# First attention's outputs stored unnormalised, their scale applied where the first branch loads them

## Chip, core and metric

The kernel runs on one core of a Trainium2 chip. The metric is device time in microseconds (us) of one execution; 2043.49 us is the median of three runs of the kernel before.

## The reference, cut to what matters

One layer of a decoder trunk on 1024 tokens of width 1024, in float32. Three token mixers A, B and C each give 512 features per token. The change touches mixer A, differential attention with four heads of 128 values each:

```python
s = jnp.einsum('bqhcd,bkhcd->cbhqk', qi, k) * scale + bias
p = jax.nn.softmax(jnp.where(mask, s, NEG_INF), axis=-1)
w = p[0] - lam * p[1]
oa = jnp.einsum('bhqk,bkhe->bqhe', w, v)
...
oa = (rms_norm(oa, diff_subln[layer]) * (1.0 - lam_init)).reshape(B, S, MIX_WIDTH)
...
y = jnp.einsum('nbsm,nmd->bsnd', branches, w_branch[layer])
gate = jax.nn.sigmoid(mg.reshape(B, S, N_BRANCH, D_MODEL))
x = x + jnp.sum(gate * y, axis=2) @ w_out[layer]
```

`rms_norm` divides each token's 128 values of a head by the root of their mean square. A per-value gain (`diff_subln`) and a constant follow.

## The kernel before

The work runs in stages on one core. Five engines work in their own order: TensorE (PE, with its weight loads PEld), VectorE (DVE), ScalarE (ACT), GpSimd (POOL) and SyncE (SP), which issues nearly all DMAs. PE's order is the order in which the code is written; the other engines' orders are set by a scheduler that simulates the program. Each engine then takes its instructions strictly in order.

Matrix products are made from a high and a low part of each operand (`split`: ScalarE copies the high part, L90, and DVE or POOL subtracts it, L91), three matmuls for each product (`mm3`, L118 to L120).

`run` goes through the stages. `mix` weaves two streams of PE work: a fine one, the steps of an attention (`pipeline`, `step`), and a dense one, the matmuls of a projection or of gates. First attention (mixer A, four heads, `items_a`) is woven with the projections of the next head. An item is a block of 256 queries of one head, so 16 items in all. Each step makes logits (L711), exponentials (`expo`, L743), transposes of the probabilities into a PSUM bank (`pblocks`, L759), and products with the values that gather in a bank `ac`.

PSUM gives two banks named `tr` in turn to whoever asks: the attention's transposes (L759), the projection's transposes (`to_state`, L558, copied out by DVE in L564 or ScalarE in L562), and the end of an item. That end works as follows. `values` copies the item's output `o`, value dimension on the partitions, out of PSUM (L861). Some steps later `by_token` (L869 to L882) transposes it to token on the partitions (L872), copies it (L874), takes each token's sum of squares (L878), adds the epsilon that was scaled by the softmax's sum (L879), raises it to the power -0.5 on POOL (L880) and multiplies (L881). Again two steps later `by_feature` (L884 to L890) transposes back (L887), applies `subln` in the copy (L889) and stores 128x256 to `od` in DRAM. The helper `late` holds these two for a number of steps.

Mixers B and C follow. The second half of mixer C's attention (`items_c`, g = 1) is woven with `first_branch`: for each half of the tokens some gates (`gates(n)`), the loads of mixer A's four heads from `od` (`operand`, L1130, then `split` to `xh`, `xl`), some more gates (`gates(m)`), and eight products with the branch's weights (`branch`), each gated and stored to `yd`. Gates go to DRAM by L1124. In this stage raw loads have two buffers (`wr`), weight parts four (`wh`, `wl`), and the tile pool `sq` still holds the projection's small tiles `y` with two buffers.

Of the kernel before, what the change touches and what calls it, by code (L numbers as in the profile page):

```python
# [11 lines left out]
F32 = mybir.dt.float32  # L12
F32R = mybir.dt.float32r
AF = mybir.ActivationFunctionType
ALU = mybir.AluOpType
AX = mybir.AxisListType

P = 128
S = 1024
# [56 lines left out]
class Kernel:  # L76
# [97 lines left out]
    def run(self):  # L174
        tc, nc, a = self.tc, self.nc, self.a
# [25 lines left out]
        self.w_n, self.wr_bufs, self.w_bufs = 396, WR, 8  # L201
        self.od = self.dram.tile([12, P, S], F32, name="od")
        self.gd = self.dram.tile([24, P, S], F32, name="gd")
        self.yd = self.dram.tile([KT, P, S], F32, name="yd")
        self.next_gate = 0
        self.mm, self.alone, self.raws = self.sc, True, []
# [112 lines left out]
    def idents(self):  # L319
        nc = self.nc  # L320
        self.cst.tile([P, 24], F32, name="gap0")
        self.ident = self.cst.tile([P, P], F32, name="ident")
        make_identity(nc, self.ident)
        self.identr = self.ca.tile([P, P], F32R, name="identr")
        nc.vector.tensor_copy(self.identr, self.ident)
        self.nhalf = self.cst.tile([P, 8], F32, name="nhalf")
        nc.vector.memset(self.nhalf, -0.5)
        self.cst.tile([P, 120], F32, name="gap1")
        self.gk = self.ca.tile([P, 3, HD], F32, name="gk")
        self.gsw = self.ca.tile([P, 2, HD], F32, name="gsw")  # L330

# [457 lines left out]
    def items_a(self, h, sta):  # L789
        nc, at = self.nc, self.at  # L790
        bias = self.bias[:, h, :]
        for qb in range(4):
            pq = [None, None]
            box = {}
# [48 lines left out]
            rows = []  # L843
# [9 lines left out]
            def values(i, ph, pl, kt, qb=qb, box=box):  # L853
                if kt + i == 0:
                    box["ac"] = self.ac()
                self.mm3(box["ac"], sta["v"][:, kt + i, 0, :], sta["v"][:, kt + i, 1, :], ph, pl,
                         kt + i == 0, kt + i == 2 * qb + 1)
                if kt + i == 2 * qb + 1:
                    box["o"] = at.tile([P, 256], F32, name="o1", tag="o1", bufs=2)
                    with self.tc.high_priority(offset=self.urgent):  # L860
                        nc.scalar.activation(box["o"], box["ac"], AF.Copy)  # L861
                return 0.33

            groups = [self.group(lambda j, kt, pq=pq: pq[j][:, kt * P:(kt + 1) * P], qb, (kt, kt + 1),
                                 lambda t, kt: kt <= t, lambda i, ph, pl, kt=kt, values=values: values(i, ph, pl, kt))
                      for kt in range(0, 2 * qb + 2, 2)]


            def by_token(box=box, qb=qb):  # L869
                pt = self.tr()  # L870
                for j in range(2):
                    nc.tensor.transpose(pt[:, j * P:(j + 1) * P], box["o"][:, j * P:(j + 1) * P], self.ident)  # L872
                o2 = box["o2"] = at.tile([P, 2, P], F32, name="o2", tag="o2", bufs=2)
                nc.scalar.activation(o2, pt[:, 0:256].rearrange("p (j e) -> p j e", e=P), AF.Copy)  # L874
                ss = at.tile([P, 2, 2], F32, name="sso", tag="sso", bufs=2)
                for j in range(2):
                    v = pt[:, j * P:(j + 1) * P]
                    nc.scalar.activation(v, v, AF.Square, accum_out=ss[:, 0, j:j + 1])  # L878
                nc.vector.scalar_tensor_tensor(ss[:, 1, :], ss[:, 0, :], 1.0 / P, box["eps"], op0=ALU.mult, op1=ALU.add)  # L879
                nc.gpsimd.tensor_tensor(ss[:, 1, :], ss[:, 1, :], self.nhalf[:, 0:2], op=ALU.pow)  # L880
                nc.vector.tensor_tensor(o2, o2, ss[:, 1, :].unsqueeze(2).to_broadcast([P, 2, P]), op=ALU.mult)  # L881
                self.late.append([2, lambda: by_feature(box, qb)])  # L882

            def by_feature(box, qb):  # L884
                pt = self.tr()
                for j in range(2):
                    nc.tensor.transpose(pt[:, j * P:(j + 1) * P], box["o2"][:, j, :], self.ident)  # L887
                o1 = at.tile([P, 256], F32, name="o1", tag="o1", bufs=2)
                nc.scalar.activation(o1, pt[:, 0:256], AF.Copy, scale=self.subln)  # L889
                nc.sync.dma_start(self.od[h, :, qb * 256:(qb + 1) * 256], o1)  # L890

            yield dict(rows=rows, groups=groups, end=[by_token])

    def head_values(self, box, dst, v, ph, pl, first, last):

# [228 lines left out]
                nc.sync.dma_start(self.gd[f, :, hs], o)  # L1124


    def operand(self, src, s, hi, lo):

        raw = self.wp.tile([P, 512], F32, name="wr", tag="wr", bufs=self.wr_bufs)
        self.nc.sync.dma_start(raw, src[:, s])  # L1130
        self.split(hi, lo, raw)


# [14 lines left out]
    def first_branch(self):  # L1148
        nc = self.nc
        for half, n, m in ((0, GATES[3], GATES[4]), (1, GATES[5], 24 - sum(GATES))):  # L1150
            s = slice(half * 512, half * 512 + 512)
            yield from self.gates(n)
            o = [self.parts(tag="x") for _ in range(4)]
            for i in range(4):
                self.operand(self.od[i], s, *o[i])
            yield from self.gates(m)
            for d in range(KT):
                w = self.weight(self.a["wbr"][0, d], 512)
                g = self.gate(self.sq, "tm", 2, 0, d, s)
                ps = self.branch(0, d, [x[0] for x in o], [x[1] for x in o], w)  # L1160
                with self.tc.high_priority(offset=self.urgent):
                    nc.vector.scalar_tensor_tensor(g, g, 1.0, ps, op0=ALU.add, op1=ALU.mult)
                nc.sync.dma_start(self.yd[d, :, s], g)
                yield 2.6
# [424 lines left out]
```

## Time and profile before

| | |
|---|---|
| runs, us | 2043.49, 2041.05, 2048.14 (median 2043.49) |
| profiled execution, us | 2045.69 |
| its span, first to last instruction | 2043.7 |
| mean granted TensorE clock | 0.98 |
| TensorE busy | 1901.7 us, 93% |
| DVE, ScalarE, POOL busy | 70%, 50%, 47% |

| stretch, us | stage |
|---|---|
| 0 to 160 | norm, first projection, compression of keys for mixer C |
| 160 to 455 | first attention (mixer A) with the projections |
| 455 to 870 | mixer B, first half of mixer C, with projections and gates |
| 870 to 1196 | second half of mixer C with gates and first branch |
| 1196 to 2044 | other branches, output product, MLP |

A row of a group reads: line, engine, operation, output tile <- input tiles, shape, count | busy us in all, mean ns of one | idle time of the engine just before them and what ended it. A row of a timeline begins with start and length in us. PE's matmuls overlap, so what one of them costs is the distance between starts, not its shown length.

### The profile page before, as it was taken

Reading aid. Unit: us, or ns where it says so; the run is one execution under the profiler, and the core shown is the slowest. Engines: PE = TensorE matmul, PEld = TensorE weight load, DVE = VectorE, ACT = ScalarE, POOL = GpSimd, SP = SyncE. Lnnn points to the kernel's source line nnn. Section 1 sums busy time; section 2 is a strip of 40 time slices with the busy share of each in tenths; the row PEclk is TensorE's granted clock in tenths of the full one; section 3 lists DMA queues with packets and bytes.
Section 4 is the critical chain, followed back from the end, with each engine's and each line's share of the span. In section 5 each row is a group of like instructions: output and inputs, shape, how many; then the busy total and the mean of one; then the engine's idle time right before and its main releaser. Section 6 shows DMA issues by size and latency. Waiting matters only on the chain. (4 is left out here: it accounts for less than half of the span.)

```text
span 2043.7 us, 30701 instructions
## 1 busy us (share of the span) xinstructions
PE 1901.7 (93%) x9838; PEld 1621.5 (79%) x9838; DVE 1423.4 (70%) x3231; ACT 1022.0 (50%) x2626; POOL 954.3 (47%) x1142
## 2 busy tenths in 40 slices
PE   7999888988799999999999899999899998999998
PEld 6888887888688888887888677787688886888876
DVE  6757777788848677648676755657755544889898
ACT  5456556666636555536555533335455544444331
POOL 4455355544352212162222227218444445789784
PEclk9999999999999999999999899999899998999999
DMA  5131022011211111212242456425444446355343
GB/s 218 51 104 52 4 55 59 26 38 37 87 28 61 56 52 51 72 33 91 68 147 77 159 198 204 147 93 161 172 167 160 144 145 247 119 167 163 124 144 114
DMA packets 122558, 219.49 MB, mean 107 GB/s; under 512 B 14420, under 2 KB 35412, under 8 KB 122396
## 3 DMA queue, kind: packets, MB, share of 16 engines
q1 hardware_dynamic: 120812, 211.75, 31.9%
q10 hardware_dynamic: 1584, 5.77, 0.9%
q8 instruction: 78, 1.28, 0.3%
q14 instruction: 84, 0.69, 0.1%
HBM read 156.59 MB, written 64.81 MB: 108 GB/s over the span
## 5 line engine op out<-in xcount | busy, mean ns | idle before, releaser
L91 POOL TENSOR_TENSOR wl<-wr,wh 128x512 fp32r<-128x512 f32 (+3 forms) x246 | 328.8, 1343 | 275.0 <-ACT wh L90 238.8
L90 ACT ACTIVATE wh<-wr 128x512 fp32r<-128x512 f32 (+3 forms) x258 | 150.3, 590 | 183.8 <-PE mm L119 124.1
L711 PE MATMUL sc<-st 128*128 128x256 f32 (+5 forms) x736 | 183.9, 344 | 25.9 <-ACT p L743 25.3
L90 ACT ACTIVATE ph<-tr 128x384 fp32r<-128x384 f32 (+3 forms) x280 | 138.4, 497 | 105.5 <-PE tr L759 87.0
L91 DVE TENSOR_TENSOR pl<-tr,ph 128x384 fp32r<-128x384 f32 (+3 forms) x280 | 155.8, 559 | 40.2 <-ACT ph L90 37.6
L756 POOL MEMSET ph<- 128x128 f32 x152 | 35.7, 235 | 291.3 <-PE ac L901 253.0
L711 PEld LDWEIGHTS sc<-st 128*128 128x128 f32 x736 | 122.8, 192 | 47.5 <-ACT p L743 38.8
L118 PE MATMUL mm<-hh,wh 128*128 128x512 f32 x384 | 158.8, 414 | 0.0
L120 PE MATMUL mm<-hh,wl 128*128 128x512 f32 x384 | 151.5, 395 | 0.0
L119 PE MATMUL mm<-hl,wh 128*128 128x512 f32 x384 | 151.4, 394 | 0.0
L119 PE MATMUL mm<-wl,wh 128*128 128x512 f32 x352 | 139.5, 396 | 9.4 <-POOL wl L91 9.4
L118 PE MATMUL mm<-wh 128*128 128x512 f32 x352 | 139.9, 398 | 8.2 <-DVE x L1471 5.3
L90 ACT ACTIVATE wh<-u 128x512 fp32r<-128x512 f32 x162 | 93.0, 620 | 106.3 <-PE mm L119 27.9
L759 PE MATMUL tr<-ident,p 128*128 128x128 f32 x792 | 129.2, 275 | 16.9 <-ACT o L889 7.8
L120 PE MATMUL mm<-wh,wl 128*128 128x512 f32 x352 | 139.1, 395 | 0.0
L743 ACT ACTIVATE p<-sc,mc 128x256 f32<-128x256 f32 (+5 forms) x200 | 106.7, 538 | 52.0 <-DVE mc L735 47.0
L901 PE MATMUL ac<-ph,st 128*128 128x256 f32 x392 | 109.8, 298 | 19.4 <-DVE ob L908 11.5
L91 POOL TENSOR_TENSOR wl<-s,wh 128x512 fp32r<-128x512 f32 x64 | 89.5, 1405 | 79.3 <-ACT wh L90 79.3
L118 PE MATMUL mm<-wh,hh 128*128 128x384 f32 (+1 forms) x320 | 117.0, 366 | 0.0
L91 DVE TENSOR_TENSOR wl<-u,wh 128x512 fp32r<-128x512 f32 x98 | 112.5, 1150 | 3.9 <-ACT wh L90 3.9
L902 PE MATMUL ac<-pl,st 128*128 128x256 f32 x392 | 106.5, 292 | 6.5 <-DVE pl L91 5.8
L91 POOL TENSOR_TENSOR wl<-u,wh 128x512 fp32r<-128x512 f32 x64 | 98.8, 1557 | 25.1 <-ACT wh L90 25.0
(311 smaller groups left out, 5771.2 us busy)
## 6 DMA issues: line engine op xcount, KB each, us to landing
ud<-u SPq DMA_DIRECT2D x112, 256.0 KB, 2.2
u<-ud SPq DMA_DIRECT2D x98, 256.0 KB, 3.3
wr<-wu SPq DMA_DIRECT2D x76, 256.0 KB, 2.8
wr<-wd SPq DMA_DIRECT2D x64, 256.0 KB, 2.9
gd<-go SPq DMA_DIRECT2D x48, 256.0 KB, 2.0
g<-gd SPq DMA_DIRECT2D x48, 256.0 KB, 3.2
wr<-wg SPq DMA_DIRECT2D x40, 256.0 KB, 2.7
wr<-wbr SPq DMA_DIRECT2D x40, 256.0 KB, 3.0
```

The source lines that it names most:

```text
L90: nc.scalar.activation(hi, src, AF.Copy)
L91: (eng or nc.vector).tensor_tensor(lo, src, hi.bitcast(F32), op=ALU.subtract)
L118: mm(out, lh, rh, start=first, stop=False, skip_group_check=more)
L119: mm(out, lh, rl, start=False, stop=False, skip_group_check=more)
L120: mm(out, ll, rh, start=False, stop=last, skip_group_check=more)
L711: self.nc.tensor.matmul(ps[:, off:off + k1 - k0], q[:, t * P:(t + 1) * P], k[:, k0:k1], start=i == 0, stop=i == 1)
L743: self.nc.scalar.activation(p, ps, AF.Exp, bias=m, scale=-1.0, accum_out=l)
L756: nc.gpsimd.memset(ph[0:rows, o:o + P].bitcast(F32), 0.0)
L759: nc.tensor.transpose(pt[0:rows, o:o + P], src, self.ident)
L901: nc.tensor.matmul(ac, v, ph, start=first, stop=False)
L902: nc.tensor.matmul(ac, v, pl, start=False, stop=last)
```

## The change

The item's output is stored to `od` as it is, right after it is copied out of PSUM. ScalarE squares it into `o2`, and a function `norms` replaces `by_token` and `by_feature`: two products of the squares with a column of ones give the sums per token, with tokens on the partitions. The epsilon and the power follow as before, and the 256 factors are stored to a new DRAM tile `rd`. `operand` loads the factors' row, spread over all partitions, in two pieces of 256, and one DVE instruction for each piece multiplies the raw operand by `subln` and by the row. `first_branch` puts the four operand loads between the matmuls of `gates(m)`, after every fourth step, where they stood ahead of them.

```diff
+        self.rd = self.dram.tile([4, S], F32, name="rd")
...
+        self.ones = self.cst.tile([P, 8], F32, name="ones")[:, 0:1]
+        nc.vector.memset(self.ones, 1.0)
...
                         nc.scalar.activation(box["o"], box["ac"], AF.Copy)
+                    o2 = box["o2"] = at.tile([P, 256], F32, name="o2", tag="o2", bufs=2)
+                    nc.scalar.activation(o2, box["o"], AF.Square)
+                    nc.sync.dma_start(self.od[h, :, qb * 256:(qb + 1) * 256], box["o"])
...
-            def by_token(box=box, qb=qb):
+            def norms(box=box, qb=qb):
                 pt = self.tr()
                 for j in range(2):
-                    nc.tensor.transpose(pt[:, j * P:(j + 1) * P], box["o"][:, j * P:(j + 1) * P], self.ident)
...
-                self.late.append([2, lambda: by_feature(box, qb)])
...
+                    nc.tensor.matmul(pt[:, j:j + 1], box["o2"][:, j * P:(j + 1) * P], self.ones, start=True, stop=True)
+                ss = at.tile([P, 2], F32, name="sso", tag="sso", bufs=2)
+                nc.vector.scalar_tensor_tensor(ss, pt[:, 0:2], 1.0 / P, box["eps"], op0=ALU.mult, op1=ALU.add)
+                nc.gpsimd.tensor_tensor(ss, ss, self.nhalf[:, 0:2], op=ALU.pow)
+                r = self.rd[h]
+                nc.sync.dma_start(bass.AP(tensor=r.tensor, offset=r.offset + qb * 256, ap=[[1, P], [P, 2]]), ss)
...
+        if rows is not None:
+            for o in (0, 256):
+                r = self.sq.tile([P, 256], F32, name="y", tag="y", bufs=2)
+                src = bass.AP(tensor=rows.tensor, offset=rows.offset + s.start + o, ap=[[0, P], [1, 256]])
+                self.nc.sync.dma_start(r, src)
+                v = raw[:, o:o + 256]
+                self.nc.vector.scalar_tensor_tensor(v, v, self.subln, r, op0=ALU.mult, op1=ALU.mult)
...
-            for i in range(4):
-                self.operand(self.od[i], s, *o[i])
-            yield from self.gates(m)
+            for k, c in enumerate(self.gates(m)):
+                if k % 4 == 3 and k // 4 < 4:
+                    self.operand(self.od[k // 4], s, *o[k // 4], self.rd[k // 4])
+                yield c
```

Lines of the changed kernel are shifted: L762 is the attention's transposes (L759 before), L714 the logits (L711), L878 the ones products, L1123 an operand's raw load (L1130 before), L1128 a load of a row piece, L1130 now the DVE product, L1117 a gate's store (L1124), L902 a store of mixer B or C (L909), L1164 a store to `yd` (L1163).

TensorE at the end of an item in the first head, where three users of the `tr` banks follow each other. Before:

```order
L119 MATMUL ac<-pl,st 128x256
L120 MATMUL ac<-ph,st 128x256
L872 MATMUL tr<-ident,o_2368 128x128 x2
L887 MATMUL tr<-ident,o_2326 128x128 x2
L759 MATMUL tr<-ident,p 128x128 x3
L711 MATMUL sc<-st 128x384 x2
```

The same place now:

```order
L119 MATMUL ac<-pl,st 128x256
L120 MATMUL ac<-ph,st 128x256
L878 MATMUL tr<-ones,o_2371 128x1 x2
L762 MATMUL tr<-ident,p 128x128 x3
L714 MATMUL sc<-st 128x384 x2
```

Two users of a bank stand where three stood; all else on TensorE keeps its order.

SyncE's DMAs around the second half's operand loads. Before, the loads from `od` stand ahead of the first of the six gate stores of this half:

```order
L1130 DMA wr<-od 128x512
L1163 DMA yd<-g 128x512
L1130 DMA wr<-od 128x512
L1137 DMA g<-gd 128x512
L1130 DMA wr<-od 128x512
L100 DMA wr<-wg 128x512 x2
L1124 DMA gd<-go 128x512
L909 DMA od<-ob 64x256
L100 DMA wr<-wbr 128x512
```

Now:

```order
L1123 DMA wr<-od 128x512
L902 DMA od<-ob 64x256
L1117 DMA gd<-go 128x512
L1123 DMA wr<-od 128x512
L1128 DMA y<-rd 128x256 x2
L1123 DMA wr<-od 128x512
L1128 DMA y<-rd 128x256 x2
L1123 DMA wr<-od 128x512
L1128 DMA y<-rd 128x256 x2
L100 DMA wr<-wbr 128x512 x2
L1117 DMA gd<-go 128x512
```

They moved behind the gate weights and the half's first two gate stores, with two row loads each (the first operand's stand far earlier), ahead of the third gate store.

DVE at the same loads, now (before, only the four splits `xl<-wr,xh` stood there):

```order
L1130 SCALAR_TENSOR_TENSOR wr<-wr,subln,y 128x256
L731 TENSOR_TENSOR mc<-mc 128x1
L738 ISA sc,mc<-sc,bias,mc 128x256
L738 ISA mc 128x1
L91 TENSOR_TENSOR xl<-wr,xh 128x512
L1130 SCALAR_TENSOR_TENSOR wr<-wr,subln,y 128x256 x2
L738 ISA sc,mc<-sc,bias,mc 128x256
```

Between the products of one operand and those of the next stand a step of the attention's minimum (L738, before L735) and the split.

More of the change, by code (lines that the diff above doesn't have):

```diff
@@ L327, in idents @@
         nc.vector.memset(self.nhalf, -0.5)
-        self.cst.tile([P, 120], F32, name="gap1")
+        self.ones = self.cst.tile([P, 8], F32, name="ones")[:, 0:1]
+        nc.vector.memset(self.ones, 1.0)
+        self.cst.tile([P, 112], F32, name="gap1")
         self.gk = self.ca.tile([P, 3, HD], F32, name="gk")
@@ L866, in items_a @@
                       for kt in range(0, 2 * qb + 2, 2)]
-            def by_token(box=box, qb=qb):
+            def norms(box=box, qb=qb):
                 pt = self.tr()
                 for j in range(2):
[L872 to L881, printed above, removed]
-                self.late.append([2, lambda: by_feature(box, qb)])
[L884 to L892, printed above, removed]
+                    nc.tensor.matmul(pt[:, j:j + 1], box["o2"][:, j * P:(j + 1) * P], self.ones, start=True, stop=True)
[4 more added lines that the diff above has]
+                nc.sync.dma_start(bass.AP(tensor=r.tensor, offset=r.offset + qb * 256, ap=[[1, P], [P, 2]]), ss)
+            yield dict(rows=rows, groups=groups, end=[norms])
     def head_values(self, box, dst, v, ph, pl, first, last):
@@ L1124, in gates, with operand @@
                 nc.sync.dma_start(self.gd[f, :, hs], o)
-    def operand(self, src, s, hi, lo):
+    def operand(self, src, s, hi, lo, rows=None):
         raw = self.wp.tile([P, 512], F32, name="wr", tag="wr", bufs=self.wr_bufs)
         self.nc.sync.dma_start(raw, src[:, s])
+        if rows is not None:
[5 more added lines that the diff above has]
+                self.nc.vector.scalar_tensor_tensor(v, v, self.subln, r, op0=ALU.mult, op1=ALU.mult)
         self.split(hi, lo, raw)
```

## Prediction

> **What bounds the kernel now.** I read the page's share of busy time first, then a table of busy time by stage, then the list of waits of TensorE in the stage that the change touches most, and last the rows of single operations that carry a price.
>
> ```profile
> span 2043.7 us, 30701 instructions
> PE 1901.7 (93%) x9838; PEld 1621.5 (79%) x9838; DVE 1423.4 (70%) x3231; ACT 1022.0 (50%) x2626; POOL 954.3 (47%) x1142
> ...
> 160.00:455.00 295.00, 262.49 (x1663) 243.21 (x1661) 227.00 (x647) 179.74 (x594) 147.02 (x238) 0.98 0.15 41
> 455.00:870.00 415.00, 386.23 (x2233) 333.80 (x2233) 297.14 (x969) 238.59 (x719) 128.20 (x285) 0.99 0.18 55
> 870.00:1125.00 255.00, 246.30 (x1375) 210.63 (x1374) 174.45 (x533) 140.22 (x398) 82.13 (x135) 1.00 0.27 84
> 1125.00:1196.00 71.00, 55.98 (x294) 46.15 (x293) 50.76 (x145) 35.98 (x97) 16.76 (x31) 0.90 0.38 119
> ```
>
> The table's columns are the stretch, its length, then the busy time of PE, PEld, DVE, ACT and POOL. TensorE bounds the kernel at 93%. Its order is written by hand, so any instruction that waits on it delays all behind it. Two stretches matter. First attention runs with the projections from about 160 to 455 us; TensorE is busy for 262.5 of 295 us, so 32.5 us of it are waits. The last attention half with gates and first branch starts near 870; up to 1125 TensorE lacks only 8.7 us and DVE is 68% busy. The stages from 1196 on get the same work in the same order, and I count nothing there.
>
> Who ends TensorE's waits in first attention (engine, line, releaser, us in total, times, longest):
>
> ```profile
> PE tr L759 <- ACT o L889: 7.8, 11, 0.8
> PE sc L711 <- ACT p L743: 7.4, 10, 1.7
> PE tr L759 <- DVE pl L91: 4.9, 5, 1.3
> PE tr L759 <- DVE st L564: 3.6, 4, 1.2
> PE tr L887 <- DVE st L564: 3.2, 3, 1.1
> PE tr L558 <- ACT o L889: 1.8, 1, 1.8
> PE tr L558 <- DVE pl L91: 1.5, 1, 1.5
> ```
>
> Most are waits for one of the two `tr` PSUM banks. ScalarE's last step of the removed chain, L889, ends 7.8 + 1.8 = 9.6 us, and the removed transposes L887 wait 3.2 us themselves. One place shows how:
>
> ```profile
> 411.28 0.44 PE L887 MATMUL tr<-ident,o 128*128 128x128 f32 x2 [1.02 <-DVE st L564]
> 412.56 0.44 PE L759 MATMUL tr<-ident,p 128*128 128x128 f32 x2 [0.84 <-ACT o L889]
> ...
> 411.75 0.38 ACT L874 ACTIVATE o<-tr 128x256 f32<-128x256 f32 x1 [0.68 <-PE tr L887]
> 412.04 0.47 ACT L889 ACTIVATE o<-tr,subln 128x256 f32<-128x256 f32 x1
> ```
>
> Three users of two banks stand in a row: the transposes of one item, those of the item before, and the attention's own. The second waits 1.02 us for a copy on DVE, the third 0.84 us for ScalarE.
>
> **The change part by part: TensorE in first attention.** Per item (16 of them) two pairs of 128x128 transposes go, and two products of 128x128 with a column of ones come.
>
> ```profile
> 182.17 0.38 PE L872 MATMUL tr<-ident,o 128*128 128x128 f32 x2
> 182.38 0.60 PE L759 MATMUL tr<-ident,p 128*128 128x128 f32 x4
> ...
> 191.40 0.46 PE L558 MATMUL tr<-identr,tm 128*128 128x128 f32 x4
> 191.70 0.35 PE L118 MATMUL ac<-ph,st 128*128 128x256 f32 x1
> ...
> 182.71 0.19 PEld L118 LDWEIGHTS mm<-wh,hh 128*128 128x128 f32 x1
> L384 PE MATMUL sc<-oh,rb x4: 481/481/495, 63.7 to 64.7; 32*20 32x384 f32 x4
> ```
>
> A shown duration is not the cost, since matmuls overlap; starts are. The pair L872 holds TensorE from 182.17 to 182.38, 0.105 us each: 64 x 0.105 = 6.7 us go. For the new ones there is no row of this form. L384 is the kernel's only plain f32 product, two matmuls in the code and four records, so each f32 product runs as two. The 32 new ones give 64 records whose moving side is one column; the weight load of 128x128 decides. Below, the L558 pitch, (191.70 - 191.40) / 4 = 0.075 us, gives 4.8; above, a whole weight load of 0.19 us with nothing overlapped gives 12.2. I take L872's 0.105, the same f32 weights: 6.7. Net 0, ends -1.9 and +5.5.
>
> The Trainium skill, "FP8 and Floating Point Precision", TensorE Precision Notes, says that true FP32 takes four passes through the array. If each pass loaded weights for itself, 128 x 0.105 = 13.4 us would stand against 6.7, and my sum would end at +2.7 instead of -4. The four records for two matmuls in this trace speak for two loads per product, so I keep 0.
>
> **Waits for the banks.** At most 9.6 (ended by L889) + 3.2 (L887's own) = 12.8 us go. The floor is 0: the L759 that stood behind L887 now takes the bank that L887 took, and can wait for the same copy L564; the bank of the new product is freed by a small DVE instruction that stands in DVE's queue, and DVE is 227.0/295 = 77% busy. TensorE arriving earlier also meets the other waits (L711 for exponentials, 7.4 us) earlier. Of 12.8 I take a little over half, -7; the ends are -12.8 and 0.
>
> **ScalarE, DVE, POOL and SP in first attention.**
>
> ```profile
> L861 ACT ACTIVATE o<-ac 128x256 f32<-128x256 f32 x16 | 6.3, 391 | 2.1 <-PE ac L120 2.0
> L874 ACT ACTIVATE o<-tr 128x256 f32<-128x256 f32 x16 | 6.1, 383 | 6.7 <-PE tr L872 3.9 <-PE tr L887 2.9
> L878 ACT ACTIVATE tr<-tr 128x128 f32<-128x128 f32 x32 | 8.7, 272 | 0.6
> L878 ACT ACTIVATION_READ_ACCUMULATOR tr<-tr 128x1 f32 x32 | 6.3, 197 | 0.0
> L889 ACT ACTIVATE o<-tr,subln 128x256 f32<-128x256 f32 x16 | 7.5, 471 | 3.5 <-DMA od<-o 2.0 <-PE tr L872 1.3
> L881 DVE TENSOR_TENSOR o<-o,sso 128x256 f32<-128x256 f32 x16 | 9.6, 601 | 1.7 <-POOL sso L880 1.6
> ```
>
> ScalarE loses 6.1 + 8.7 + 6.3 + 7.5 = 28.6 us and gains 16 squares at about L861's 0.391 = 6.3: 22 us less of 179.7. DVE loses 9.6 us of 227.0; its small step on the sums and POOL's power stay. None of this is TensorE's own time; it pays only through the waits above, and I add nothing for it. SP keeps 16 stores of the outputs, now sent earlier, and gets 16 stores of 1 KB behind POOL's power. Weight loads queue behind each of these, but the store it replaces waited for ScalarE at the end of an even longer chain, so 0; were that cover gone, a late weight load would show as a wait of ScalarE's split on DMA, then of TensorE. Nobody reads the sums until after 900 us.
>
> **The operand loads under the last attention half.** Each of eight loads gets two DVE products of 128x256 and two loads of 128 KB that spread one row over 128 partitions.
>
> ```profile
> L835 DVE SCALAR_TENSOR_TENSOR p<-pb,l,p 128x256 f32<-128x256 f32 x4 | 2.4, 607 | 0.1
> L536 DVE TENSOR_TENSOR y<-raw,ssq 128x256 f32<-128x256 f32 x32 | 15.9, 496 | 8.1 <-POOL ssq L126 8.1
> L735 DVE CUSTOM_DVE_ANT_0 sc<-sc,bias,mc 128x256 f32<-128x256 f32 x96 | 46.3, 490 | 10.7 <-PE sc L711 5.9 <-ACT st L562 0.7 <-DVE mc L728 0.7
> 922.86 0.69 DVE L91 TENSOR_TENSOR xl<-wr,xh 128x512 fp32r<-128x512 f32 x1
> DMA to landing us min/median/max: 2.3/3.8/4.5
> 920.00:945.00 25.00, 23.82 (x131) 19.14 (x130) 22.13 (x77) 18.44 (x56) 9.87 (x12) 1.00 0.41 125
> 1075.00:1095.00 20.00, 19.09 (x109) 16.46 (x108) 13.52 (x46) 11.58 (x33) 3.56 (x7) 1.00 0.19 60
> ...
> 1078.63 0.33 SPq L1124 DMA_DIRECT2D gd<-go  x1
> ...
> 1088.58 0.33 SPq L1124 DMA_DIRECT2D gd<-go  x1
> ...
> 1118.17 0.39 PE L118 MATMUL mm<-xh,wh 128*128 128x512 f32 x1
> ```
>
> L835 is the same operation and size: 8 x 0.607 = 4.9 us of DVE per half (8 x 0.496 = 4.0 by the plainer L536). The first half's loads fall where DVE already works 22.13 of 25 us, the second's where it works 13.52 of 20. Idle DVE time covers 2.9 and 6.5 us: 2.0 us stay over in the first half, none in the second. The landing time is that of the `bias` loads (L403), the nearest of this size and row length. The row tiles have two buffers, so loads of the next operand are issued only after a product of this one has read its tile. By the order a second product, an attention step like L735 and a split like L91 lie between the two: 0.607 + 0.490 + 0.69 = 1.8 us. With the median landing of 3.8 DVE stands still for 2.0 us, with 2.3 for 0.5. Three operands per half wait so: 3 to 12 us in both halves, of which idle time takes much. What is queued behind the waiting product on DVE is the softmax, for which ScalarE and then TensorE wait; TensorE has gate matmuls and a lag of two steps in between. On TensorE I take 2.0 + 1 = +3. The ends are 0, all hidden, and (4.9 x 2 + 12) - 9.4 = +12.4, all late DVE time passed on. The products need the second half's operands at 1118.17; their loads now stand in SP's queue between the gate stores of 1078.63 and 1088.58, so some 30 us of cover stay, and their place in the queue costs 0. Gate weights and stores queue behind them on SP and have about the length of a gate half, 10 us, to spare.
>
> **Sum.** 0 - 7 + 3 = -4 us. The profiled execution took 2045.69 us around a span of 2043.7, 2.2 above the median of the three runs, 2043.49. So it would come to 2041.7, and the median to 2039.5.
>
> **Rivals.** First: all bank waits go and DVE hides the rest. For it: the waits come in the same place item after item, and ScalarE and DVE both lose work. Against: waits in a fixed order tend to come back one step on. -12.8 + 0 gives 2043.49 - 12.8 = 2030.7.
>
> Second, slower: DVE's in-order wait for the row tiles becomes the bound. Its place are operands two to four of each half, its price 2.0 us a wait plus the products, +12.4, with only -4 from first attention: +8.4, or 2051.9. It decides once the loads land later than about 3.8 us there. For it: DVE at 22.13 of 25 us. Against: TensorE waits little in that stretch and has gate matmuls to run.
>
> Third: the ones products cost TensorE as much as is saved, with four weight loads each. 128 x 0.105 - 6.7 = +6.7, and -7 + 6.7 + 3 = +2.7 gives 2046.2, no change. For it: no row has such a product of 128x128. Against: L384's two records per product. It is the Trainium skill's four passes taken as four loads ("FP8 and Floating Point Precision", TensorE Precision Notes).
>
> **How the numbers follow.** About 0.3%, or 6.1 us, is what this measurement can tell from no change. My forecast gets 0.40 and lies inside that; the third rival 0.06, also inside; the full gain 0.36, faster; the DVE bound 0.18, slower. So faster 0.36, same 0.46, slower 0.18. The forecast's own range is 2037 to 2046. To leave out no more than 2 in 10 the range takes in both rivals down to 2029 and up to 2051.
>
> **What would show it.** Right: no more TensorE waits ended by ScalarE's last step in first attention, the sum of waits there near 25 instead of 32.5 us, starts of the ones products about 0.1 us apart per record, ScalarE near 158 us busy there. In the stretch from 920 to 960 a few us of new TensorE waits, ended by exponentials or by DVE's splits. Wrong: DVE waiting more than 2 us at a time for a DMA of the row tiles; TensorE waiting for the new squares; or bank waits of the old size with another name.

## The result, and the profile after

The changed kernel takes 2056.92 us (median of 10 runs, 2049.74 to 2061.79) against 2041.53 us of the kernel before beside it (10 runs). The ratio is 1.0081, 95% interval 1.0060 to 1.0101: slower by some 16 us. The forecast was 2039.5 us, with 2029 to 2051 as its range; the result lies above both.

The two stretches of the prediction's table, in the changed kernel (same columns: PE, PEld, DVE, ACT, POOL busy, then granted clock and DMA share):

```profile
160.00:455.00 295.00, 258.92 (x1641) 244.57 (x1639) 209.83 (x617) 161.14 (x509) 143.62 (x233) 0.95 0.22 40
870.00:1125.00 255.00, 239.60 (x1306) 204.28 (x1305) 174.15 (x525) 133.50 (x378) 78.10 (x131) 0.97 0.28 86
```

ScalarE and DVE lost the work that was to go (ScalarE 179.7 to 161.1 us, DVE 227.0 to 209.8), but TensorE is busy for less of the time than before (258.9 of 295 us against 262.5), at a lower granted clock (0.95 against 0.98). So the chain became lighter and the stretch longer. The waits of TensorE from 160 to 456 us say how:

```profile
PE tr L762 <- DVE st L567: 23.6, 7, 6.8
PE sc L714 <- ACT p L746: 4.7, 8, 1.0
PE tr L762 <- DVE pl L91: 3.9, 1, 3.9
PE ac L894 <- DVE ssq L125: 1.2, 1, 1.2
```

The waits that L889 ended are gone, as the change promises. In their place stand seven waits for DVE's copy L567, 23.6 us together and up to 6.8 us at a time, where the longest in the prediction's rows was 1.8 us. DVE is not short of time, so the question is what DVE was waiting for. The timeline around one of the long waits (start, length, engine, what, in brackets the idle time before and who ended it):

```profile
256.61 0.37 SPq L883 DMA_DIRECT2D rd<-sso  x1
...
257.60 3.97 SPq L100 DMA_DIRECT2D wr<-wa  x3
...
262.77 0.50 PE L878 MATMUL tr<-ones,o 128*128 128x1 f32 x4
...
266.11 0.52 ACT L90 ACTIVATE wh<-wr 128x384 fp32r<-128x384 f32 x1 [6.87 <-DMA wr<-wa]
...
266.54 0.47 ACT L523 ACTIVATE raw<-mm 128x384 f32<-128x384 f32 x1
...
267.26 0.35 ACT L746 ACTIVATE p<-sc,m 128x128 f32<-128x128 f32 x1
...
267.73 0.56 DVE L840 SCALAR_TENSOR_TENSOR eps<-l 128x1 f32<-128x1 f32 x1 [5.97 <-ACT p L746]
...
269.29 0.67 DVE L567 CAST st<-tr 128x512 fp32r<-128x512 f32 x1
...
270.02 1.11 PE L762 MATMUL tr<-ident,p 128*128 128x128 f32 x4 [6.74 <-DVE st L567]
```

Read it from the bottom. TensorE waits 6.74 us for a bank; the copy that frees it, L567, is late because DVE stood 5.97 us at L840 for an exponential; the exponential is late because ScalarE stood 6.87 us at the high part of a weight tile whose load had not landed; that load was sent at 257.60 (the first of the three in its row), the next thing on SyncE's queue behind the new store `rd<-sso` of 256.61, and ScalarE could take it 8.5 us later. The store's time from issue to landing (minimum, median, maximum), and then, from the list of DMA issues, the medians of one of the weight loads and of the store:

```profile
DMA to landing us min/median/max: 7.8/8.1/9.4
```

```profile
wr<-wa SPq DMA_DIRECT2D x32, 192.0 KB, 4.5
...
rd<-sso SPq DMA_DIRECT2D x16, 1.0 KB, 8.1
```

The store of 1 KB takes 8.1 us; the outputs' store of 128 KB takes 1.7. Its 1 KB is 256 pieces of 4 bytes, since consecutive tokens lie on different partitions. From 160 to 456 us 24 weight loads and 12 of these stores have a recorded landing: the 11 loads that were sent while one of the stores was in flight took 7.0 to 11.1 us (median 8.5), the others 2.6 in the median. ScalarE's waits for weight loads from 160 to 456 us, first in the changed kernel, then before:

```profile
ACT wh L90 <- DMA wr<-wa: 17.1, 7, 6.9
ACT wh L90 <- DMA wr<-wb: 16.5, 5, 7.5
```

```profile
ACT wh L90 <- DMA wr<-wb: 3.4, 5, 1.4
ACT wh L90 <- DMA wr<-wa: 1.3, 3, 0.8
```

33.6 us against 4.7. This is the first part of the loss. The second is the operands' part from 918 us on, where ScalarE and TensorE wait at one of the moved operand loads:

```profile
1092.58 0.48 DVE L1130 SCALAR_TENSOR_TENSOR wr<-wr,subln,y 128x256 f32<-128x256 f32 x1 [0.41 <-DMA y<-rd]
...
1093.10 0.63 ACT L90 ACTIVATE xh<-wr 128x512 fp32r<-128x512 f32 x1 [3.08 <-DVE wr L1130]
1093.63 0.63 ACT L746 ACTIVATE p<-sc,mc 128x448 f32<-128x448 f32 x1
...
1094.41 0.58 PE L714 MATMUL sc<-st 128*128 128x256 f32 x1 [4.62 <-ACT p L746]
```

ScalarE's copy `xh` waits 3.08 us for DVE's product, the softmax's exponential is queued right behind it, and TensorE waits 4.62 us for the exponential.

Matching the same TensorE instructions in two traces shows how far one runs behind the other. From before's 160 us to its 600 us the changed kernel loses 5.1 us, from 600 to 920 nothing, from 920 to 1320 it loses 9.9, and after that 0.8. The 5.1 is a gain and a larger loss in one sum; the first experiment parts them.

### The profile page after: what moved, and what is told of

It reads as the page before. It is cut to its first block, busy times and chain, and to the rows that moved or that the text cites. A ratio compares the mean times of both kernels' runs of the same rounds, so it can differ in the third digit from the quotient of the medians.

```text
span 2058.4 us, 30688 instructions
## 1 busy us (share of the span) xinstructions
PE 1905.6 (93%) x9838; PEld 1630.0 (79%) x9838; DVE 1417.6 (69%) x3232; ACT 1005.4 (49%) x2546; POOL 951.4 (46%) x1142
## 2 busy tenths in 40 slices
DMA packets 129214, 221.60 MB, mean 108 GB/s; under 512 B 19028, under 2 KB 42068, under 8 KB 129052
## 5 line engine op out<-in xcount | busy, mean ns | idle before, releaser
L91 POOL TENSOR_TENSOR wl<-wr,wh 128x512 fp32r<-128x512 f32 (+3 forms) x246 | 328.5, 1341 | 303.2 <-ACT wh L90 260.0
L714 PE MATMUL sc<-st 128*128 128x256 f32 (+5 forms) x736 | 185.9, 347 | 29.4 <-ACT p L746 29.0
L91 DVE TENSOR_TENSOR pl<-tr,ph 128x384 fp32r<-128x384 f32 (+3 forms) x280 | 155.5, 559 | 48.7 <-ACT ph L90 46.7
L759 POOL MEMSET ph<- 128x128 f32 x152 | 34.6, 227 | 298.3 <-PE ac L894 245.8
L714 PEld LDWEIGHTS sc<-st 128*128 128x128 f32 x736 | 125.0, 196 | 50.8 <-ACT p L746 41.8
L762 PE MATMUL tr<-ident,p 128*128 128x128 f32 x792 | 132.8, 281 | 27.7 <-DVE st L567 23.6
L91 POOL TENSOR_TENSOR wl<-s,wh 128x512 fp32r<-128x512 f32 x64 | 89.1, 1400 | 77.8 <-ACT wh L90 77.8
L762 PEld LDWEIGHTS tr<-ident,p 128*128 128x128 f32 x792 | 95.7, 145 | 29.6 <-DVE st L567 24.9
L91 DVE TENSOR_TENSOR wl<-u,wh 128x512 fp32r<-128x512 f32 x98 | 112.0, 1145 | 4.0 <-ACT wh L90 4.0
```

The costliest lines, as they stand in the source:

```text
L91: (eng or nc.vector).tensor_tensor(lo, src, hi.bitcast(F32), op=ALU.subtract)
L714: self.nc.tensor.matmul(ps[:, off:off + k1 - k0], q[:, t * P:(t + 1) * P], k[:, k0:k1], start=i == 0, stop=i == 1)
L759: nc.gpsimd.memset(ph[0:rows, o:o + P].bitcast(F32), 0.0)
L762: nc.tensor.transpose(pt[0:rows, o:o + P], src, self.ident)
```

## The experiments

Each kernel was timed against the kernel before on the same chip. "A" is what the stretch from 160 to 600 us gains or loses against the same instructions of before, "C" the stretch from 920 to 1320 us; these come from one trace each. Kernels that are alike in a stretch show how far such a figure repeats: A of the three with the packed store per item is -21.8, -18.8 and -20.1, of the seven with one per head -21.7 to -29.3, of the two with the unchanged store +5.1 and +1.0; C of the six with the changed kernel's operand loads is 7.1 to 11.3.

```
kernel                                      median   ratio to before (95%)      A      C
changed kernel                             2056.92   1.0081 (1.0060-1.0101)   +5.1   +9.9
 without the factors' stores               2024.23   0.9925 (0.9910-0.9939)  -27.5  +11.3
 stores on ScalarE's DMA queue             2054.78   1.0074 (1.0061-1.0087)   -0.1  +10.8
 stores of 128 x 8 bytes                   2034.80   0.9970 (0.9958-0.9982)  -18.2   +9.9
 packed store per item                     2029.89   0.9950 (0.9935-0.9965)  -21.8   +7.1
 packed store per head                     2023.45   0.9914 (0.9897-0.9932)  -29.3   +7.4
 without row loads and products            2044.38   1.0024 (1.0011-1.0037)   +1.0   +3.9
packed per item, work in three             2029.82   0.9944 (0.9927-0.9961)  -18.8   +5.2
packed per item, products on POOL          2034.75   0.9971 (0.9956-0.9986)  -20.1  +11.5
packed per head, rows loaded once          2025.41   0.9921 (0.9905-0.9937)  -24.5   +5.9
 operands at the old place                 2029.50   0.9943 (0.9925-0.9960)  -25.5  +14.5
 spread over eight steps                   2030.79   0.9945 (0.9920-0.9969)  -27.0  +14.4
 spread, products on POOL                  2020.46   0.9893 (0.9875-0.9910)  -25.1   +3.6
 spread, own tiles                         2017.18   0.9903 (0.9888-0.9919)  -26.7    0.0
 spread, own tiles, products on POOL       2014.62   0.9886 (0.9871-0.9901)  -21.7   -1.2
```

### The store: left out, elsewhere, packed, in larger pieces

**Without it.** The edit:

```diff
-                nc.sync.dma_start(bass.AP(tensor=r.tensor, offset=r.offset + qb * 256, ap=[[1, P], [P, 2]]), ss)
+        nc.sync.dma_start(self.rd, a["x"][0:4, 0:S])     # once, in bias_vectors
```

> Changed kernel without the 16 stores of the factors; the row tensor is written once, near 64 us, from the input, so the factors are left out of the result. Nothing takes the store's place. Theory A: time falls by 7 to 12 us against the changed kernel, 2045 to 2050 us, and TensorE's idle time from 160 to 455 us falls from about 36 us to 25 us, as first forecast. Theory B: no change, 2055 to 2059 us.

It took 2024.23 us, 32 us below the changed kernel by the ratios ((1.0081 - 0.9925) x 2041.53), where theory A expected 7 to 12. The mechanism is A's, its size was not. The rows of the stretch between the same TensorE instructions, of before, of the changed kernel and of the one without the store:

```profile
160.00:500.00 340.00, 299.90 (x1905) 278.21 (x1904) 266.43 (x783) 209.06 (x699) 170.55 (x300) 0.98 0.15 40
```

```profile
159.00:504.50 345.50, 301.21 (x1905) 283.65 (x1904) 252.90 (x767) 191.45 (x618) 169.77 (x300) 0.95 0.21 39
```

```profile
155.75:469.30 313.55, 291.26 (x1905) 274.17 (x1904) 251.05 (x767) 191.51 (x619) 169.27 (x300) 0.99 0.16 43
```

TensorE's idle time is 40.1 us before, 44.3 in the changed kernel, 22.3 without the store; its busy time 299.9, 301.2 and 291.3 for the same number of matmul records. So without the store the new first attention saves 17.8 us of waits and 8.6 us of busy time, and the store costs 22.0 and 9.9 of them again. Between the last two kernels TensorE's instructions are the same, so the 9.9 us are not fewer or cheaper matmuls. Busy time moves with the granted clock: stretches of 1 us ahead of and behind the wait that ends at 270 us, first the changed kernel, then before (the granted clock is the third figure from the end):

```profile
263.00:264.00 1.00, 0.27 (x3) 0.19 (x2) 0.00 (x0) 0.00 (x0) 0.00 (x0) 1.00 0.44 26
...
265.00:266.00 1.00, 0.00 (x0) 0.00 (x0) 0.00 (x0) 0.00 (x0) 0.00 (x0) 1.00 0.15 17
266.00:267.00 1.00, 0.00 (x0) 0.00 (x0) 0.00 (x0) 0.89 (x2) 0.29 (x1) 0.51 0.21 65
...
269.00:270.00 1.00, 0.00 (x0) 0.00 (x0) 0.79 (x3) 0.47 (x3) 1.00 (x2) 0.50 1.05 392
270.00:271.00 1.00, 0.98 (x5) 0.99 (x6) 0.93 (x4) 0.23 (x1) 0.86 (x2) 0.50 0.71 259
271.00:272.00 1.00, 1.00 (x5) 1.00 (x5) 0.67 (x2) 0.83 (x3) 1.00 (x2) 0.50 0.75 204
```

```profile
264.00:265.00 1.00, 0.40 (x2) 0.20 (x2) 1.00 (x2) 0.00 (x0) 1.00 (x2) 1.00 0.86 187
265.00:266.00 1.00, 0.16 (x2) 0.13 (x2) 1.00 (x2) 0.93 (x4) 1.00 (x2) 1.00 0.98 202
...
268.00:269.00 1.00, 1.00 (x6) 0.90 (x5) 0.67 (x3) 0.30 (x2) 1.00 (x3) 0.50 0.97 340
269.00:270.00 1.00, 1.00 (x7) 1.00 (x6) 0.43 (x2) 0.54 (x3) 0.30 (x1) 0.50 0.75 269
```

In the changed kernel the clock halves some 3 us after TensorE falls idle, and it stays so for over 2 us after work is back. Before, waits of 1.0 and 0.8 us within 2 us of each other were enough, here and again near 412 us; near 344 us a single wait of 1.8 us was. Without the store only one 10 us stretch of the first attention has a clock under 0.95. An estimate from such rows over the three stretches, busy time times what the clock lacks of 1.00: 6.8 us before, 12.6 in the changed kernel, 1.6 without the store. So the clock makes about 5 of the 8.6 us, and all of the 9.9 within the estimate's error. The Trainium skill, "TensorE: Matmul & The Clock Gate", Part 1, states half clock after a window of about 3.4 us that it calls idle; the changed kernel's rows agree, and before's show that a window 60 to 84% idle for 2 us did it too.

**On another queue.** The same 256 pieces from ScalarE's DMA queue, two steps later:

```diff
-                nc.sync.dma_start(bass.AP(..., ap=[[1, P], [P, 2]]), ss)
+                def store(ss=ss):
+                    nc.scalar.dma_start(bass.AP(..., ap=[[1, P], [P, 2]]), ss)
+                self.late.append([2, store])
```

> Changed kernel with the 16 four-byte stores sent from ScalarE's DMA queue, two steps later (so that ScalarE doesn't wait for POOL's power), instead of from SP's. Theory A1 (the store holds only loads behind it in its own queue): the weight loads on SP's queue land in 2 to 3 us again and the time falls by 6 to 10 us, 2047 to 2051 us. Theory A2 (it holds the DMA engines or the memory, whatever the queue): weight loads sent within 8 us of a store still land in 8 to 11 us, time as in the changed kernel, 2054 to 2060 us. Theory B: as A2 in time, but with loads on time.

2054.78 us, ratio 1.0074: theory A2. Store and weight loads, the same view:

```profile
wr<-wa SPq DMA_DIRECT2D x32, 192.0 KB, 4.8
...
rd<-sso ACTq DMA_DIRECT2D x16, 1.0 KB, 7.7
```

The store still takes 7.7 us. The weight loads stay on SyncE's queue, in which it no longer stands, and stay late: those sent while such a store was in flight took 6.1 to 16.7 us (10 loads, median 8.6), the others 2.6 in the median. It is no matter of the place in a queue. The Trainium skill, "DMA: Bandwidth & Descriptors", "Issuing engines are not separate DMA queues", says that all issuers end on the same 16 engines; this run agrees.

**Larger pieces.** 128 pieces of 8 bytes, the same 1 KB:

```diff
-                ...ap=[[1, P], [P, 2]]), ss)
+                ...ap=[[2, P], [1, 2]]), ss)
```

> Changed kernel with the two factors of a token side by side in the row tensor, so that each store is 128 elements of 8 bytes instead of 256 of 4 bytes, the same 1 KB (the factors then meet the wrong tokens in the result). Theory A (the store is paid by the element): it lands in 4 to 5 us instead of 8, the late weight loads come 3 to 5 us less late, and the time is about half way to the kernel without the store, 2036 to 2046 us. Theory A3 (any store of elements this small holds the engines as long, whatever their number): it lands in 7 us or more, 2053 to 2059 us.

2034.80 us, 22 us below the changed kernel, a little under theory A's range. The page's counts of DMA packets under 512 bytes, 19028 in the changed kernel and 16980 here, differ by 2048 = 16 x 128, as they should. The store lands in about a third of the time, where theory A expected a half:

```profile
rd<-sso SPq DMA_DIRECT2D x16, 1.0 KB, 2.9
```

A3 falls. That cost goes by the number of pieces alone is not shown either, since half the pieces saved 5.2 of 8.1 us.

**Packed.** Per item, and then per head (there `ss` is a slice of one 128x8 tile, and the step runs once):

```diff
-                r = self.rd[h]
-                nc.sync.dma_start(bass.AP(..., ap=[[1, P], [P, 2]]), ss)
+                self.late.append([2, lambda: packed(ss, qb)])
+            def packed(ss, qb):
+                pt = self.tr()
+                nc.tensor.transpose(pt[0:2, 0:P], ss, self.ident)
+                row = at.tile([2, P], F32, name="row", tag="row", bufs=1)
+                nc.vector.tensor_copy(row, pt[0:2, 0:P])
+                r = self.rd[h]
+                nc.sync.dma_start(bass.AP(..., ap=[[P, 2], [1, P]]), row)
```

> Changed kernel with one edit: two steps later the 128x2 factors are transposed on TensorE to two rows of 128, copied by DVE, and stored as 2 elements of 512 bytes instead of 256 of 4 bytes. Theory A (the store of 256 four-byte elements takes 8 us to land and holds up the weight loads that were sent behind it, so ScalarE's split, the exponentials and DVE's copies come late): the store lands in about 2 us, weight loads behind it in 2 to 3 us, the three TensorE waits of 6.2 to 6.8 us on a tr bank go, and the time falls by 6 to 11 us against the changed kernel, to 2046 to 2051 us. Theory B (the tr waits are DVE being late by its own work, with a user of the banks that only changed its name): waits and time as in the changed kernel or, with 16 more users of the tr banks, 1 to 3 us more, 2056 to 2060 us.

> The packed kernel with the factors of a whole head (8 columns) collected and transposed, copied and stored once per head instead of once per item: 4 transposes, copies and stores instead of 16. Theory E (the 5.7 us between the packed kernel, 2029.9, and the kernel without store, 2024.2, are the third user of the tr banks and its DVE copy): 2025 to 2028 us. Theory F (they are the stores and the weight loads behind them): also fewer stores here, but the waits of TensorE on banks freed by DVE's copy of the row would already be few in the packed kernel; 2028 to 2031 us if neither matters and the difference is spread over the rest.

2029.89 and 2023.45 us: both are faster than the kernel before, and by more than theory A expected, since the lighter chain saves more than the prediction's sum had (see below). Theory B falls with the long waits. Per head against per item saves 0.9950 - 0.9914 = 0.36%, 7.3 us, more than theory E's 2 to 5. Each of the 12 steps saved is a use of a tr bank, a transpose, a copy and a store at once, 0.6 us in all, so this run doesn't part E from F. With one store per head no wait of TensorE on a tr bank is over 1.5 us, in the stretch that answers to 160 to 500:

```profile
...
PE sc L714 <- ACT p L746: 5.3, 8, 1.4
PE tr L762 <- DVE st L567: 3.8, 4, 1.5
...
PE tr L762 <- DVE sso L883: 1.5, 3, 0.6
PE tr L890 <- DVE st L567: 1.4, 2, 1.2
```

### The operands: what the 10 us in the last attention half are

**Without the scale.** No row loads, no products:

```diff
-                    self.operand(self.od[k // 4], s, *o[k // 4], self.rd[k // 4])
+                    self.operand(self.od[k // 4], s, *o[k // 4])
```

> Changed kernel with the first branch's operand loads at their new places but without the row loads and DVE products (the scale is left out of the result). Theory C (the row loads and products cost the last attention half 10 to 13 us, because ScalarE's split waits for them in order with the softmax's exponentials behind it): 2043 to 2048 us, with no ScalarE wait over 1 us on that product's line. Theory D (what costs there is the place of the loads in SP's queue, between the gates' loads and stores): at most 3 us less than the changed kernel, 2053 to 2057 us.

2044.38 us, 11.6 us less ((1.0081 - 1.0024) x 2041.53); the two intervals together leave about 7 to 16. Theory C, though by the traces only 6 us of it lie in stretch C; 4 lie in A, where the two kernels are alike and a trace repeats no better than that. D may have a share: stretch C still loses 3.9 us with loads alone, in the one trace.

**Four edits on the packed kernels.** First the operand's work in three parts (loads at the first of four gate steps, products at the third, split at the fourth; a gate step is one `mm3`, three matmuls, and is what the expectations call a pair):

```diff
-                if k % 4 == 3 and k // 4 < 4:
-                    self.operand(self.od[k // 4], s, *o[k // 4], self.rd[k // 4])
+                i, j = k // 4, k % 4
+                if i < 4 and j == 0:
+                    t = self.operand_load(self.od[i], s, self.rd[i])
+                if i < 4 and j == 2:
+                    self.operand_scale(*t)
+                if i < 4 and j == 3:
+                    self.split(*o[i], t[0])
```

> The packed kernel with each operand's step in three: loads at the first of four matmul pairs, DVE products at the third, ScalarE's and DVE's split at the fourth, instead of all at the fourth. Theory C (what costs in the last attention half is that DVE and ScalarE wait in order for the landing of the rows and for the products, with the softmax behind them): the waits of DVE on the rows' DMA go and the time falls by 3 to 7 us, 2023 to 2027 us. Theory G (it is the 9.8 us of additional DVE work): no change, 2028 to 2032 us.

Second, with all of it at every fourth step as in the changed kernel, the products on POOL:

```diff
-                self.nc.vector.scalar_tensor_tensor(v, v, self.subln, r, op0=ALU.mult, op1=ALU.mult)
-        self.split(hi, lo, raw)
+                self.nc.gpsimd.tensor_tensor(v, v, r, op=ALU.mult)
+        self.nc.scalar.activation(hi, raw, AF.Copy, scale=self.subln)
+        self.nc.vector.scalar_tensor_tensor(lo, raw, self.subln, hi.bitcast(F32), op0=ALU.mult, op1=ALU.subtract)
```

> The packed kernel with the row products on POOL (128x256 twice per operand) in place of DVE; the gain per feature goes into ScalarE's copy of the high part as its scale and into DVE's subtraction, which add no instruction. All at the old place in the order. Theory G (9.8 us of DVE work is the cost): the time falls by 4 to 8 us, 2022 to 2026 us. Theory C (ScalarE waits in order for landing and product, whichever engine multiplies): no change or a little more, since POOL's product is the slower one, 2028 to 2034 us.

Third, the rows loaded once per half:

```diff
-                r = self.sq.tile([P, 256], F32, name="y", tag="y", bufs=2)
-                ...
-                self.nc.sync.dma_start(r, src)
+                r = rows[o // 256]        # two tiles "r", loaded at k == 0 from self.rd[0]
```

> The kernel with one packed store per head (2023.4 us) with the rows loaded once per half, for head 0, into two tiles of their own and used for all four operands (heads 1 to 3 are then scaled by the wrong factors): all DVE products stay, 12 of 16 row loads go. Theory C (DVE's products wait in order for the rows to land, ScalarE's copy of the high part waits for the products, and the softmax's exponentials stand behind it): 5 to 8 us less, 2015 to 2019 us, and TensorE's longest wait for exponentials there, 5.5 us, falls under 2.5 us. Theory G (the 9.8 us of DVE work): 2021 to 2025 us.

Fourth, the operands back ahead of the gates:

```diff
-            for k, c in enumerate(self.gates(m)):
-                if k % 4 == 3 and k // 4 < 4:
-                    self.operand(self.od[k // 4], s, *o[k // 4], self.rd[k // 4])
-                yield c
+            for i in range(4):
+                self.operand(self.od[i], s, *o[i], self.rd[i])
+            yield from self.gates(m)
```

> The kernel with one packed store per head, with the four operands of a half loaded, scaled and split one behind the other ahead of the second group of gates, where the kernel before has its loads. Theory H (the place inside the gates is the cost, since ScalarE's copies there stand in the softmax's way): 2 to 5 us less, 2018 to 2021 us. Theory C: with two row tiles for four operands DVE waits for three landings of 2.5 to 3.5 us in a row, with ScalarE behind it, 2 to 6 us more, 2025 to 2030 us.

Three parts: no change, as theory G says; but DVE still waited 4.3 us for the rows (4.7 in the packed kernel), so the edit didn't remove the wait that it was to remove, and tests neither theory. Products on POOL: 0.21% slower than on DVE (the intervals overlap a little), against G: taking DVE's products away, 8.1 us by the packed kernel's trace and not 9.8, gained nothing. Rows loaded once: no change, against C as I had put it; TensorE's wait of 5.5 us is still there, at 5.3 us, though DVE's longest wait for a DMA on the products' line is 1.0 us:

```profile
1055.78 0.88 DVE L1138 SCALAR_TENSOR_TENSOR wr<-wr,subln,r 128x256 f32<-128x256 f32 x2 [0.42 <-issue]
...
1056.69 0.63 ACT L90 ACTIVATE xh<-wr 128x512 fp32r<-128x512 f32 x1 [2.72 <-DVE wr L1138]
...
1059.07 0.80 PE L714 MATMUL sc<-st 128*128 128x256 f32 x2 [5.34 <-ACT p L746]
```

So the landing of the rows is not it, and DVE's work alone doesn't look like it. Old place: 0.29% slower (C's sign; the intervals overlap by little); its trace, of a run 7.7 us above the median, has one wait of 8 us of TensorE behind the gates' weights; H falls.

What the four leave, by argument so far, is the operand itself. Its tile `wr` is one of two that the gates' weights use too, so its load is sent late, and whoever multiplies or splits it waits in order.

**Spread, then with own tiles.** The operand's work over eight gate steps (loads at the first, products at the fifth, split at the eighth), under the longer group of gates, with two tiles for the rows alone; then the same with the products on POOL, as above:

```diff
-                i, j = k // 4, k % 4
+                i, j = k // 8, k % 8      # loads at j == 0, products at 4, split at 7
```

> The kernel with one packed store per head, with the operands spread over eight matmul pairs each instead of four, under the longer of the half's two groups of gates: loads at the first pair, DVE products at the fifth, split at the eighth; the rows get two tiles of their own. Theory C: landings lie behind them when the products' turn comes, 4 to 8 us less, 2015 to 2020 us. Theory G: no change, 2021 to 2025 us. That four pairs were too short for this is what the run with loads, products and split at the first, third and fourth of four pairs has left open.

> The same spreading over eight pairs, with the row products on POOL and the gain per feature folded into ScalarE's copy and DVE's subtraction. Theory C: about the time of the spread kernel with DVE products, within 2 us of it, since nobody waits for the products any more. Theory G: 4 to 8 us less than that one.

Against the kernel with one packed store per head, spreading lost 0.31% with products on DVE and gained 0.21% with them on POOL; each interval overlaps that kernel's a little, the two do not overlap each other's. Both theories missed: with DVE's products neither expected a loss, and POOL's are 0.52%, 10.6 us, below them, more than G's 4 to 8 and against C's 2. Who made DVE wait on the products' line in the first of the two:

```profile
DVE wr L1150 <- issue: 3.2, 2, 2.4
DVE wr L1150 <- DMA wr<-od: 3.1, 2, 2.8
DVE wr L1150 <- DMA r<-rd: 1.7, 2, 1.0
DVE wr L1150 <- DMA wr<-wg: 1.2, 1, 1.2
```

The longest named wait is for the operand, `wr<-od`, not for the row, and the two waits of the first row, which the profile puts down to nobody, end 0.1 us after an operand landed. On POOL the same wait is longer, 10.9 us in three times, but no exponential is queued there: TensorE's waits for exponentials from 885 to 1110 us are 2.5 us with POOL's products, 10.8 with DVE's. This fits a cost that hangs on the place of the wait more than on its length; DVE's work is gone in this pair too, and the last edit bears on that. It gives operands and rows two tiles each of their own and, by the code, loads an operand twelve or thirteen gate steps ahead of its products, the first of each half four:

```diff
-        raw = self.wp.tile([P, 512], F32, name="wr", tag="wr", bufs=self.wr_bufs)
+        raw = self.sq.tile([P, 512], F32, name="oraw", tag="oraw", bufs=2)
+        r = self.sq.tile([P, 512], F32, name="r", tag="r", bufs=2)
```

> The spread kernel with DVE products (2030.8 us) with two 512-wide tiles of their own for the operands and two for the rows, so that each operand's loads are sent at least eight pairs of matmuls ahead of its products and share no tile with the gates' weights. Theory C2 (DVE waits in order for the operand's own landing, ScalarE's copy for the product, and the softmax stands behind both): DVE's waits for a DMA on the product's line fall from 6 us to under 1 us, TensorE's waits for exponentials there from 10.8 to about 3 us, and the time by 8 to 14 us, to 2016 to 2022 us. Theory G (the 9.8 us of product work in DVE's queue): 2027 to 2032 us.

> The same with one product of 128x512 on POOL per operand, the gain per feature folded into ScalarE's copy and DVE's subtraction. Theory C2: within 3 us of the kernel above, 2015 to 2021 us, since in both no queue of the softmax waits for a landing. Theory G: 2016 to 2021 us, 8 us or more below the kernel above.

2017.18 us with DVE's products: theory C2, 0.42% or 8.6 us below the spread kernel (2030.79). Stretch C costs nothing any more (0.0 us). TensorE's waits for exponentials from 885 to 1110 us fell from 10.8 to 5.1 us (3 were expected), DVE's for the operand there to 1.9 (under 1 was expected):

```profile
PE sc L714 <- ACT p L746: 5.1, 5, 1.8
```

```profile
DVE oraw L1146 <- DMA oraw<-od: 1.9, 4, 1.1
```

More changed than the edit says. Once the tiles were free, the scheduler moved the loads and products of the first two operands of each half far ahead, those of the first half to here:

```profile
537.68 0.88 DVE L1146 SCALAR_TENSOR_TENSOR oraw<-oraw,subln,r 128x256 f32<-128x256 f32 x2 [2.55 <-DMA r<-rd]
540.13 1.45 DVE L1146 SCALAR_TENSOR_TENSOR oraw<-oraw,subln,r 128x256 f32<-128x256 f32 x2 [1.57 <-DMA r<-rd]
```

DVE still waits 4.1 us there, for the rows, but TensorE's longest wait from 520 to 560 us is 0.7 us. The second half's first two are multiplied at 899 to 901 us, more than 100 us before ScalarE copies them. So about three quarters of the 9.4 us of products are left in stretch C, at no cost to it; the head start that did this is larger than the one that was written, and the run doesn't part it from the separate tiles.

With POOL's products it is 2014.62 us; the ratios 0.9903 and 0.9886 have overlapping intervals, so G's 8 us are not there. These kernels are 1.0 to 1.1% faster than the one before. Against the kernel with one packed store per head (0.9914) they are 0.1 and 0.3% faster, and their intervals overlap its interval: what is clear is the gain over the spread kernel with DVE's products, not that over this one. With POOL's products the tiles of their own gained nothing clear (0.9886 against 0.9893), as is to be expected where no exponential is queued behind the wait.

## Why the prediction was wrong, point by point

- **The swap of transposes for products with ones, 0.** Nothing speaks against it. The four records of an item are over within 0.50 us (row 262.77), where the four transposes were priced at 4 x 0.105 = 0.42. The third rival, four loads per product, doesn't show: the trace has 64 weight loads at L878, not 128.
- **SyncE's 16 stores, "so 0". This is the step that failed.** The prediction compared the new store with the one it replaced by the time at which it is sent, and by its 1 KB. It never priced its landing, nor what that does to the loads sent meanwhile. The run without it puts the price at 32 us, and the other queue, the larger pieces and the packed rows put it down to the small pieces and not to the place in a queue. The sentence on a lost cover named the sign rightly (ScalarE's split on DMA, then TensorE), but gave no number, so the range did not hold it. The warning was in the diff, 256 pieces of 4 bytes. No row of before has a store in such pieces; the nearest, the load of `subln` in 128 pieces of 4 bytes, took 4.9 us for 0.5 KB, though it stands among the kernel's first loads, and could have bounded the term.
- **Bank waits, -7, ends -12.8 and 0.** Also mis-sized, on the other side. Without the store idle time fell by 17.8 us. The end of 12.8 counted only waits that the removed instructions end or have themselves; before, the `tr` waits put down to other instructions (L91 and L564, 10 us in the quoted rows) stood on the same two banks. And 8.6 us of busy time went too, which the prediction did not have: waits cost a second time by the clock, some 5 of the 8.6 us by the estimate above. What the rest is no run has parted, nor how the saved waits divide between fewer bank users and less work for ScalarE and DVE.
- **Operand loads, +3, ends 0 and +12.4.** 9.9 us by the trace, within the ends, three times the value taken, though the products themselves took 8.1 us and not 9.8. The second rival had place and sign (waits in DVE's order pass to the softmax), but put them down to two row tiles. No wait of DVE for a row in the changed kernel is over 1.6 us, and 12 of 16 row loads fewer gained nothing. What the runs point to is the operand's late load, in two tiles shared with weights, and ScalarE's copy, which waits in order for the product with the exponentials behind it. "Idle time takes much" failed: ScalarE's idle 3.08 us at `xh` covered nothing for the exponential queued behind.
- **The sum.** -4 was to be 0 - 7 + 3. Measured: first attention -26.4 without the store (340 against 313.55 us), the store +32, the operands +10; a large gain, and a larger loss from the one line counted at nothing. Without the stores the kernel gains 15 us ((1 - 0.9925) x 2041.53) where the sum had 4. The upper end, 2051, left out the second rival's own 2051.9.

## What to carry to other kernels

Price a new DMA by its pieces and by when it lands, not by its bytes: turn a per-partition column into rows before it is stored. Ask which loads are sent while it is in flight and who waits in order for them; another issuing queue was no cure here. And give a load that a softmax's engine will wait for a tile of its own and a head start, or put the wait on an engine that has nothing urgent behind it. After an edit look in the trace where the scheduler has put the work: it may not stand where the code has it.

## What the runs showed of the hardware

- A store of 256 pieces of 4 bytes took 8.1 us to land (7.7 from ScalarE's queue), and weight loads of 192 and 198 KB sent meanwhile took 8.5 us in the median (8.6) instead of 2.6; 128 pieces of 8 bytes took 2.9.
- The granted clock went to 0.50 about 3 us after TensorE fell idle (263.3 to 266 us in the changed kernel), and stayed there over 2 us once it worked again. In the kernel before it did so too where single waits were about 1 us long (1.0 and 0.8). So the store's 22.0 us of waits cost 9.9 us of busy time besides.
